# Moving the tensor operations of GpSimd (POOL) to VectorE (DVE) in the last two thirds of a transformer step: output projection and SwiGLU feed-forward

## The chip, the cores and the metric

The program runs on one core of one Trainium2 chip, in one launch. The metric is the device time of one execution in microseconds; lower is better. A core has a matrix engine (PE), a vector engine (DVE), a scalar engine (ACT), a programmable engine (POOL) and a queue engine (SP), each working through its own list of instructions in order, and DMA queues between HBM and the on-chip memory SBUF. Matrix products land in a separate memory, PSUM, from which DVE and ACT read them. An instruction that waits for another engine holds up everything behind it on its own engine.

## The reference

The reference is one inference step of one trunk layer for 128 context tokens and 1024 latent tokens (together T = 1152), width 1024, all in float32. Only its second half matters here; the first (projections, attention, mLSTM scans) is not touched.

```
out = (g_a * (att @ w_o_mla) + g_b * (hm @ w_o_mlstm)) @ w_out
x = x + gt1 * out
h = rmsnorm(x, g_norm_ffn) * (1.0 + sc2) + sh2
a, u = split(h @ w_ffn_in, 2)                  # 2 x 2816 columns
x = x + gt2 * ((silu(a) * u) @ w_ffn_out)
y = rmsnorm(x, g_final)
```

## The kernel before

**Number format.** Every float32 operand of a matrix product is split into a high part (ACT rounds it, method `hi`, line 69) and a low part (DVE subtracts, method `lo`, line 75), and `mm3` (lines 98 to 100) adds three products, high x high, high x low and low x high, so PE's matmuls come in threes on these lines. One `lo` is a DVE subtraction with both inputs in SBUF, and it has to follow its `hi`.

**Layout.** Features lie on the 128 partitions and tokens along the free dimension. The 1152 tokens are two groups g of 576 (`GT`), and each group two halves j of 288 (`HT`); a matmul has 288 columns.

**Stages touched.** They follow one another in this order.

- `merge` (from line 1527): for each feature block it multiplies the attention branch's product by its gate (line 1565), adds the mLSTM branch (line 1566, on POOL) and splits the sum into the operand y of the output projection.
- `w_out` (one call a group): eight feature blocks, two PSUM tiles each of 288 tokens. Each is turned into the new residual stream (`residual`, line 1657) and its square is added to `acc` for the norm (`sq_acc`, line 156, on POOL).
- `h2_ops` (one call a group): `row_rstd` sums `acc` over the partitions (PE, line 135), takes the reciprocal root in a chain of 12 tiny dependent DVE instructions (lines 117 to 123), builds three diagonal tiles `dg` (DVE, line 141), spreads them over the partitions (PE, line 145) and copies them to SBUF (ACT, line 146). Then line 1616 (DVE) scales the four 128x1152 blocks of x, line 1622 (ACT) applies the modulation, lines 1634 to 1644 (POOL) form four differences, and seven operands B11, T1, T2, T3, B22, T4, B21 are split (ACT `th`, DVE `tl`).
- `ffn_in`: the first feed-forward product, in Winograd's form of Strassen's scheme: seven products instead of eight on a 2x2 block pattern. For a weight pair p, `w_ops` makes four sums or differences of weight blocks (lines 1676, 1677, 1682, 1686, on POOL) and seven splits; `pair` runs seven groups of 12 matmuls a token group and combines the PSUM results in seven DVE or ACT instructions (lines 1702 and 1714). ACT applies silu, line 1747 multiplies (POOL), and the result goes to HBM. The 22 pairs come as 28 calls: the first six for g = 0 alone, then the same six for g = 1, then sixteen for both groups.
- `prep`: from the thirteenth call on it forms four sums of the second weight matrix per piece (lines 1772 to 1776, POOL) in 24 pieces, through one load buffer `pr` and one result buffer `ps`, and stores them to HBM as `d_w`.
- `out_ops` and `ffn_out`: the second product, again seven products on a 2x2 pattern, per group. `out_ops` loads the hidden activations, forms 12 differences a group (line 1816, POOL) and splits them; `out_w` splits the weights of each step (three `hi` and three `lo`: 512, 512 and 384 wide); a step is 33 matmuls into one PSUM tile, and there are 28 steps a group. `final` scales the output by the last norm (line 1888, POOL and DVE).

**What sets the order.** The tile framework places the instructions of every engine in an order that it works out for the whole program when the program is built; moving an instruction to another engine can move others too. Buffers are rings: split weights have six tiles (tag `wo`), raw weights four (`wr`), so the splits can run ahead of PE by six tiles: six groups of 12 matmuls in `ffn_in`, two steps in `ffn_out`. PE's products have six PSUM banks. Loads and stores go through SP's queue in order.

Of the kernel before, what the change touches and what calls it, by code (L numbers as in the profile page):

```python
# [14 lines left out]
ALU = mybir.AluOpType  # L15
# [6 lines left out]
KD = 8  # L22
# [26 lines left out]
HT = GT // 2  # L49
# [7 lines left out]
class K:  # L57
# [231 lines left out]
    def inputs(self):  # L289
# [9 lines left out]
        self.wp = self.w2.enter_context(self.pool("w"))  # L299
        self.wb = (4, 4)  # L300
        self.ub = 5
        pp = self.pp = ps.enter_context(self.tc.tile_pool(name="ps1", bufs=1, space=PSUM, reuse_waits="tile"))
# [1227 lines left out]
    def merge(self):  # L1530
# [8 lines left out]
        with pool("ma") as ap:  # L1539
# [8 lines left out]
            for i, (f, g) in enumerate(todo):  # L1548
# [12 lines left out]
                for c in (2 * g, 2 * g + 1):  # L1561
                    self.products(f, c, (3,) if f < 2 else range(4))
                    t = slice(c % 2 * HT, c % 2 * HT + HT)
                    yt = y[g][f][0][:, :, t]
                    nc.vector.tensor_mul(sa[:, t], sa[:, t], self.ps.pop((f, c))[:, :HT])
                    nc.gpsimd.tensor_tensor(t2[:, t], t2[:, t], sa[:, t], op=ALU.add)
                    self.hi(yt[:, 0], t2[:, t])
                    self.lo(yt[:, 1], t2[:, t], yt[:, 0])
# [3 lines left out]
        self.wp = es.enter_context(pool("w2"))  # L1572
        self.wb = (4, 6)
        ar = es.enter_context(pool("ar"))
        self.sp = es.enter_context(pool("st"))
# [9 lines left out]
    def w_out(self, g, y, w0):  # L1585
# [5 lines left out]
        for f in range(KD):  # L1591
# [4 lines left out]
            def evac(p, c0, cw):  # L1596
                b = blk[f // 4][c0 // HT][0]
                self.residual(b[:, f % 4], p, xo[:, c0:c0 + cw], self.mod2[:, 0, f], g * GT + c0, cw)
                self.sq_acc(acc[:, c0:c0 + cw], b[:, f % 4], f == 0, sp, cw, "u2", self.ub, nc.gpsimd)
                nc.sync.dma_start(self.d_x1[f, :, g * GT + c0:g * GT + c0 + cw], b[:, f % 4])  # L1600
# [5 lines left out]
    def h2_ops(self, g, blk, acc):  # L1606

        nc = self.nc
        V, G = nc.vector, nc.gpsimd
        self.row_rstd(acc, acc, D, self.sp, self.pp, "m6", chunks=[(0, HT), (HT, HT)])  # L1610
# [22 lines left out]
        split("B11", b11)  # L1633
        G.tensor_tensor(t1, b12, b11, op=ALU.subtract)
        self.free(s11)
        split("T1", t1)
        G.tensor_tensor(b12, b22, b12, op=ALU.subtract)
        G.tensor_tensor(t1, b22, t1, op=ALU.subtract)
        split("T2", t1)
# [3 lines left out]
        self.free(s22)  # L1643
        G.tensor_tensor(t1, b21, t1, op=ALU.subtract)
        split("T4", t1)
# [17 lines left out]
    def w_ops(self, ra, ru):  # L1663

        nc, wp = self.nc, self.wp
        G = nc.gpsimd
        a11, a12, a21, a22 = ra[:, 0:4], ra[:, 4:8], ru[:, 0:4], ru[:, 4:8]
# [67 lines left out]
    def ffn_in(self, p, groups, last):  # L1735
# [8 lines left out]
        def done(g):  # L1744
            sa, uu = t[g]
            nc.scalar.activation(sa, sa, AF.Silu)
            nc.gpsimd.tensor_tensor(uu, uu, sa, op=ALU.mult)
            nc.sync.dma_start(self.d_g[p, :, g * GT:(g + 1) * GT], uu)
# [8 lines left out]
    def prep(self):  # L1757

        nc, sp = self.nc, self.sp
        G = nc.gpsimd  # L1760
        for p in range(KD // 2):
# [20 lines left out]
    def out_ops(self, g):  # L1782

        nc = self.nc
        G = nc.gpsimd
        B = {}
# [86 lines left out]
    def ffn_out(self):  # L1873
# [3 lines left out]
        for g in range(2):  # L1877
# [3 lines left out]
            def final(j):  # L1881
# [3 lines left out]
                for p in range(KD // 2):  # L1885
                    x = D[p][0][:, j::2]
                    e, r = (nc.vector, bc[:, :HT]) if j == 0 and p < KD // 2 - 1 else (nc.gpsimd, rbc)
                    e.tensor_tensor(x, x, r.unsqueeze(1).broadcast_to([P, 2, HT]), op=ALU.mult)
                    c = g * GT + j * HT
                    ((nc.sync, nc.scalar)[p % 2] if g else nc.scalar).dma_start(self.o["yT"][2 * p:2 * p + 2, :, c:c + HT].rearrange("f p t -> p f t"), D[p][0][:, j::2])  # L1890
# [205 lines left out]
```

## Time and profile before

| what | value |
|---|---|
| median of 3 runs | 2201.28 us (2199.71 to 2201.73) |
| profiled execution | 2201.13 us |
| its span (first to last instruction) | 2199.4 us |
| busy share of the span | PE 94%, DVE 70%, ACT 43%, POOL 45% |

The profile counts an engine as busy from an instruction's start to its end as recorded. The window view gives busy time and number of instructions per engine in a stretch of the span; the group view gives count and mean duration per line and shape; the timeline shows single instructions, with the idle time before them and what ended it in square brackets. Line numbers are those of the kernel before.

### The profile page before, as it was taken

The page shows a single profiled execution, that of the slowest core. Times are in us where ns is not written, and L with a number is a line of the kernel's source. Part 1 is how long each engine was busy: PE and PEld are TensorE (multiplying, and loading weights), DVE is VectorE, ACT ScalarE, POOL GpSimd, SP SyncE. Part 2 cuts the span into 40 slices and gives each one's busy share as a digit, 9 for nine tenths or more (in the row PEclk, how much of TensorE's full clock was granted, in tenths as well). Part 3 has the DMA queues.
Part 4 walks back from the last instruction along what each step waited for, and adds up shares of the span by engine and source line. Part 5 has one row for each costly group of instructions (what it writes and reads, how often), then busy time and mean ns, then how long its engine had stood idle before and what let it go on. Part 6 is the DMA issues. An engine that isn't in the chain of part 4 may idle for free.

```text
span 2199.4 us, 36807 instructions
## 1 busy us (share of the span) xinstructions
PE 2057.0 (94%) x13495; PEld 1873.4 (85%) x13495; DVE 1528.7 (70%) x2700; ACT 935.4 (43%) x1850; POOL 996.6 (45%) x766
## 2 busy tenths in 40 slices
PE   7899989999989888999999999889999999989897
PEld 3689989989978775667776899879999999989897
DVE  3846656988744977566664648899645555799895
ACT  3533334555455534333433335544322222456464
POOL 0622124667435414444446535576776733421501
PEclk9999999999989997999999999899999999999898
DMA  8332335555489685222224664223556512557664
GB/s 314 103 120 83 104 99 162 164 175 187 143 284 326 198 271 153 70 78 71 84 72 116 209 206 145 76 95 123 189 171 196 176 61 85 173 168 253 220 203 129
DMA packets 233795, 343.89 MB, mean 156 GB/s; under 512 B 20079, under 2 KB 166735, under 8 KB 232463
## 3 DMA queue, kind: packets, MB, share of 16 engines
q1 hardware_dynamic: 225070, 331.88, 47.3%
q0 software_dynamic: 4848, 6.06, 1.1%
q10 hardware_dynamic: 3696, 3.61, 0.5%
q8 instruction: 106, 1.74, 0.3%
q14 instruction: 75, 0.61, 0.1%
HBM read 253.69 MB, written 87.80 MB: 155 GB/s over the span
## 4 chain that ended last, share of the span: by engine, by line
PE 47%; DVE 11%; DMA 8%; POOL 6%; issue 5%; ACT 1%; SPq 1%; DVEq 0%; POOLq 0%; ACTq 0%
PE mm L98 11%; PE mm L100 11%; PE mm L99 11%; DVE wo L75 4%; PE pv L1476 3%; DMA pr<-w_fo 3%; PE st L98 2%; PE st L99 1%; PE st L100 1%; PE mx L1398 1%; DVE sm L1400 1%; PE p L1102 1%; PE p L1107 1%; PE p L1104 1%; POOL ps L1773 1%
## 5 line engine op out<-in xcount | busy, mean ns | idle before, releaser
L100 PE MATMUL mm<-th,wo 128*128 128x288 f32 x1840 | 547.3, 298 | 15.1 <-DVE wo L75 14.8
L98 PE MATMUL mm<-th,wo 128*128 128x288 f32 x1840 | 548.7, 298 | 3.0 <-DVE zo L1702 1.1
L99 PE MATMUL mm<-tl,wo 128*128 128x288 f32 x1840 | 547.0, 297 | 0.0
L100 PEld LDWEIGHTS mm<-th,wo 128*128 128x128 f32 x1840 | 349.6, 190 | 19.2 <-DVE wo L75 18.6
L75 DVE TENSOR_TENSOR wo<-wr,wo 128x512 fp32r<-128x512 f32 (+1 forms) x317 | 315.0, 1009 | 54.5 <-ACT wo L69 51.7
L98 PEld LDWEIGHTS mm<-th,wo 128*128 128x128 f32 x1840 | 348.6, 189 | 4.9 <-issue 1.6
L99 PEld LDWEIGHTS mm<-tl,wo 128*128 128x128 f32 x1840 | 349.2, 190 | 0.1
L69 ACT ACTIVATE wo<-wr 128x512 fp32r<-128x512 f32 (+1 forms) x317 | 187.5, 608 | 141.6 <-PE mm L100 62.5
L75 DVE TENSOR_TENSOR wo<-ws,wo 128x512 fp32r<-128x512 f32 x188 | 187.9, 1002 | 64.8 <-ACT wo L69 64.7
L69 ACT ACTIVATE wo<-ws 128x512 fp32r<-128x512 f32 x188 | 116.5, 626 | 270.8 <-PE mm L100 158.1
L1445 POOL TENSOR_TENSOR es<-es,p 128x512 f32<-128x512 f32 x112 | 157.1, 1402 | 91.0 <-ACT p L1438 87.2
L100 PE MATMUL mm<-xh,wo 128*128 128x288 f32 x616 | 184.5, 301 | 9.0 <-DVE wo L75 8.9
L99 PE MATMUL mm<-xl,wo 128*128 128x288 f32 x616 | 184.6, 300 | 0.0
L98 PE MATMUL mm<-xh,wo 128*128 128x288 f32 x616 | 183.9, 299 | 0.2 <-ACT wo L69 0.2
L1686 POOL TENSOR_TENSOR ws<-wr,ws 128x512 f32<-128x512 f32 x47 | 61.8, 1316 | 226.6 <-DVE wo L75 221.2
L1438 ACT ACTIVATE p<-st 128x512 f32<-128x512 f32 (+1 forms) x152 | 87.6, 578 | 158.0 <-PE st L100 146.4
L1400 DVE TENSOR_REDUCE sm<-mx 128x1 f32<-128x384 f32 (+1 forms) x200 | 99.1, 539 | 66.0 <-PE mx L1398 65.1
L98 PE MATMUL mm<-B,wo 128*128 128x288 f32 x456 | 134.8, 296 | 2.2 <-DVE zo L1702 1.3
L100 PE MATMUL mm<-B,wo 128*128 128x288 f32 x456 | 134.8, 296 | 0.0
L99 PE MATMUL mm<-B,wo 128*128 128x288 f32 x456 | 134.8, 296 | 0.0
L722 POOL TENSOR_TENSOR wm<-wm,sr 128x512 f32<-128x512 f32 x64 | 100.8, 1578 | 65.4 <-DVE mj L721 63.4
L100 PEld LDWEIGHTS mm<-xh,wo 128*128 128x128 f32 x616 | 118.0, 192 | 11.5 <-DVE wo L75 11.2
(436 smaller groups left out, 5067.5 us busy)
## 6 DMA issues: line engine op xcount, KB each, us to landing
wr<-w_ff SPq DMA_DIRECT2D x56, 512.0 KB
wm<-wm SPq DMA_DIRECT2D x32, 512.0 KB
wr<-d_w SPq DMA_DIRECT2D x32, 512.0 KB
d_z<-zo SPq DMA_DIRECT2D x48, 288.0 KB
d_g<-uu SPq DMA_DIRECT2D x44, 288.0 KB
wr<-w_big SPq DMA_DIRECT2D x24, 512.0 KB
wr<-w_fo SPq DMA_DIRECT2D x24, 512.0 KB
pr<-w_fo SPq DMA_DIRECT2D x40, 256.0 KB
```

Source lines behind the costliest of these rows:

```text
L69: i = self.nc.scalar.activation(out, in_, AF.Copy)
L75: return self.nc.vector.tensor_sub(out, in_, f32v(hi)).ins
L98: mm(out, lhs[0], rhs[0], start=first, stop=False)
L99: mm(out, lhs[0], rhs[1], start=False, stop=False)
L100: self.pe = mm(out, lhs[1], rhs[0], start=False, stop=last).ins
L722: nc.gpsimd.tensor_tensor(w[:, n], w[:, n], sr[:, 1], op=ALU.mult)
L1102: self.pe = mm(p1, A[:, h], V[:, h], start=True, stop=not carried).ins
L1400: self.iv = nc.vector.tensor_reduce(sm[:, t, j:j + 1], s[:, :kc], axis=AX.X, op=ALU.max, negate=True).ins
L1438: self.ia = nc.scalar.activation(p[:, :n], st[:, :n], AF.Exp).ins
L1445: nc.gpsimd.tensor_tensor(U["sum"], U["sum"], p, op=ALU.add)
L1476: self.pe = nc.tensor.matmul(pv[g * AV:(g + 1) * AV, q0:q0 + w], v[:, kb[c]], U["P"][c][:, q0:q0 + w], start=c < 2, stop=c == U["nc"] - 1, ...
L1686: G.tensor_tensor(s4, a12, s2, op=ALU.subtract)
```

## The change

All tensor operations that POOL did from `merge` on go to DVE: the additions in `merge`, the sums of squares in `w_out`, the four differences in `h2_ops`, the weight sums of `w_ops` (through a field `G`, which is POOL in the earlier stages and DVE from here), the silu product, the sums of `prep`, the differences of `out_ops` and the scalings of `final`, except one scaling in the last group that stays on POOL. What is computed stays the same.

```diff
@@ inputs
         self.wb = (4, 4)
+        self.G = self.nc.gpsimd
         self.ub = 5
@@ merge
-                    nc.gpsimd.tensor_tensor(t2[:, t], t2[:, t], sa[:, t], op=ALU.add)
+                    nc.vector.tensor_add(t2[:, t], t2[:, t], sa[:, t])
...
         self.wb = (4, 6)
+        self.G = nc.vector
@@ w_out
-                self.sq_acc(acc[:, c0:c0 + cw], b[:, f % 4], f == 0, sp, cw, "u2", self.ub, nc.gpsimd)
+                self.sq_acc(acc[:, c0:c0 + cw], b[:, f % 4], f == 0, sp, cw, "u2", self.ub)
@@ h2_ops
-        G.tensor_tensor(t1, b12, b11, op=ALU.subtract)
+        V.tensor_tensor(t1, b12, b11, op=ALU.subtract)
...
-        G.tensor_tensor(b12, b22, b12, op=ALU.subtract)
-        G.tensor_tensor(t1, b22, t1, op=ALU.subtract)
+        V.tensor_tensor(b12, b22, b12, op=ALU.subtract)
+        V.tensor_tensor(t1, b22, t1, op=ALU.subtract)
...
-        G.tensor_tensor(t1, b21, t1, op=ALU.subtract)
+        V.tensor_tensor(t1, b21, t1, op=ALU.subtract)
@@ w_ops
-        G = nc.gpsimd
+        G = self.G
@@ ffn_in
-            nc.gpsimd.tensor_tensor(uu, uu, sa, op=ALU.mult)
+            nc.vector.tensor_mul(uu, uu, sa)
@@ prep
-        G = nc.gpsimd
+        G = nc.vector
@@ out_ops
-        G = nc.gpsimd
+        G = nc.vector
@@ ffn_out
-                    e, r = (nc.vector, bc[:, :HT]) if j == 0 and p < KD // 2 - 1 else (nc.gpsimd, rbc)
+                    e, r = (nc.gpsimd, rbc) if g and j == 0 and p == KD // 2 - 1 else (nc.vector, rbc if j else bc[:, :HT])
```

Up to the products of `merge` the engines' lists are the same. Behind them two places matter below. In the changed kernel, lines from 1576 on carry a number higher by two.

The first place is PE's list where the feed-forward part goes over from group 0 to group 1. `m6_2592` is the spread reciprocal root of group 1's second half of tokens (`row_rstd` in `h2_ops`), made from the diagonal tiles `dg_2591`. The products `mm_2757`, `mm_2760` and `mm_2763` are the first three of group 1, with the operands B11, T2 (`th_2598`) and T1 (`th_2596`, `tl_2597`). Before:

```order
L100 MATMUL mm_2672_14518<-th_2506_13501,wo_2671_14515 128x288
L145 MATMUL m6_2592_14114<-dg_2591_14110,ones_65 128x128 x2
L145 MATMUL m6_2592_14114<-dg_2591_14110,ones_65 128x32
L98 MATMUL mm_2672_14518<-th_2506_13501,wo_2671_14515 128x288
L99 MATMUL mm_2672_14518<-tl_2507_13502,wo_2671_14515 128x288
```

In the changed kernel:

```order
L99 MATMUL mm_2757_15017<-tl_2595_14141,wo_2756_15014 128x288
L100 MATMUL mm_2757_15017<-th_2594_14140,wo_2756_15014 128x288
L145 MATMUL m6_2592_14114<-dg_2591_14110,ones_65 128x128 x2
L145 MATMUL m6_2592_14114<-dg_2591_14110,ones_65 128x32
L98 MATMUL mm_2760_15035<-th_2598_14151,wo_2759_15032 128x288
L98 MATMUL mm_2763_15053<-th_2596_14145,wo_2762_15050 128x288
```

The spread stood in the third call for group 0, 306 rows ahead of the first matmul on T2; now it stands directly in front of that matmul, behind all of group 0's calls.

DVE's list at the same place, before. `x1_2515` and `x1_2517` are group 1's residual blocks of the second half of tokens, which line 1616 scales.

```order
L1702 TENSOR_TENSOR uu_2645_14372<-uu_2645_14372,mm_2655_14433 128x288
L75 TENSOR_TENSOR wo_2673_14533<-wr_2656_14450,wo_2673_14533 128x512
L141 TENSOR_SCALAR dg_2591_14110<-ident_60,y_2589_14096 128x128 x3
L1702 TENSOR_TENSOR u2_2665_14492<-m1_2662_14474,mm_2664_14479 128x288
L75 TENSOR_TENSOR wo_2676_14552<-ws_2675_14550,wo_2676_14552 128x512
L75 TENSOR_TENSOR wo_2678_14569<-wr_2657_14452,wo_2678_14569 128x512
L75 TENSOR_TENSOR wo_2684_14597<-wr_2680_14589,wo_2684_14597 128x512
L1702 TENSOR_TENSOR sa_2668_14510<-u2_2665_14492,mm_2667_14497 128x288
L1616 TENSOR_TENSOR x1_2515_13519<-x1_2515_13519,acc_2518_13522 128x1152
L1616 TENSOR_TENSOR x1_2517_13521<-x1_2517_13521,acc_2518_13522 128x1152
```

In the changed kernel:

```order
L1749 TENSOR_TENSOR uu_2741_14928<-uu_2741_14928,sa_2740_14927 128x576
L122 TENSOR_TENSOR t_2590_14097<-t_2590_14097,v_2588_14095 128x3
L123 SCALAR_TENSOR_TENSOR y_2589_14096<-t_2590_14097,y_2589_14096 128x3
L141 TENSOR_SCALAR dg_2591_14110<-ident_60,y_2589_14096 128x128 x3
L1618 TENSOR_TENSOR x1_2515_13519<-x1_2515_13519,acc_2518_13522 128x1152
L1618 TENSOR_TENSOR x1_2517_13521<-x1_2517_13521,acc_2518_13522 128x1152
L1636 TENSOR_TENSOR t1_2593_14139<-x1_2515_13519,x1_2514_13518 128x1152
L1639 TENSOR_TENSOR x1_2515_13519<-x1_2517_13521,x1_2515_13519 128x1152
L75 TENSOR_TENSOR tl_2597_14146<-t1_2593_14139,th_2596_14145 128x1152
L75 TENSOR_TENSOR tl_2603_14160<-x1_2517_13521,th_2602_14159 128x1152
L1640 TENSOR_TENSOR t1_2593_14139<-x1_2517_13521,t1_2593_14139 128x1152
L75 TENSOR_TENSOR tl_2601_14156<-x1_2515_13519,th_2600_14155 128x1152
```

The diagonals moved from the second call for group 0 to a place behind the silu product of its sixth and last call (`uu_2741`), and the four differences and the operand splits, which were spread over POOL's and DVE's lists, now follow in one block.

The second place is the change from the first to the second product. Before, POOL's list has the differences of group 0's hidden activations and the last two silu products in one run, while DVE's list at that time holds splits only:

```order
L1747 TENSOR_TENSOR uu_3491_19832<-uu_3491_19832,sa_3490_19831 128x576
L1816 TENSOR_TENSOR t1_3510_19931<-gr_3539_20077,t1_3510_19931 128x1152
L1816 TENSOR_TENSOR gr_3504_19895<-gr_3539_20077,gr_3504_19895 128x1152
L1747 TENSOR_TENSOR uu_3494_19848<-uu_3494_19848,sa_3493_19847 128x576
L1816 TENSOR_TENSOR t1_3509_19930<-gr_3538_20075,t1_3509_19930 128x1152
L1816 TENSOR_TENSOR gr_3503_19893<-gr_3538_20075,gr_3503_19893 128x1152
```

In the changed kernel DVE's list has:

```order
L1818 TENSOR_TENSOR t1_3510_19931<-gr_3539_20077,t1_3510_19931 128x1152
L1818 TENSOR_TENSOR gr_3504_19895<-gr_3539_20077,gr_3504_19895 128x1152
L1704 TENSOR_TENSOR uu_3494_19848<-uu_3494_19848,mm_3520_19993 128x288
L75 TENSOR_TENSOR wo_3545_20093<-wr_3533_20029,wo_3545_20093 128x384
L1818 TENSOR_TENSOR t1_3509_19930<-gr_3538_20075,t1_3509_19930 128x1152
L1818 TENSOR_TENSOR gr_3503_19893<-gr_3538_20075,gr_3503_19893 128x1152
L75 TENSOR_TENSOR wo_3552_20142<-wr_3541_20083,wo_3552_20142 128x512
L1749 TENSOR_TENSOR uu_3491_19832<-uu_3491_19832,sa_3490_19831 128x576
```

The same operations now stand between the weight splits (`wo`) that PE's next steps need, on the engine that makes those splits.

More of the change, by code (lines that the diff above doesn't have):

```diff
@@ L1608, in h2_ops @@
         nc = self.nc
-        V, G = nc.vector, nc.gpsimd
+        V = nc.vector
         self.row_rstd(acc, acc, D, self.sp, self.pp, "m6", chunks=[(0, HT), (HT, HT)])
```

## The prediction

> **What bounds the kernel now.** I read the page's first part, then the window view with its matmul counts from `merge` to the end, then the waits of PE in the stretches that fall short, and last what DVE and POOL do in them. Columns of the window view: length, then busy time and number of instructions of PE, PEld, DVE, ACT and POOL, granted PE clock, DMA share, GB/s.
>
> ```profile
> PE 2057.0 (94%) x13495; PEld 1873.4 (85%) x13495; DVE 1528.7 (70%) x2700; ACT 935.4 (43%) x1850; POOL 996.6 (45%) x766
> ```
> ```profile
> 1240.00:1370.00 130.00, 130.00 (x987) 130.00 (x986) 85.10 (x143) 56.03 (x104) 61.34 (x52) 1.00 0.61 188
> 1375.00:1475.00 100.00, 80.25 (x524) 76.19 (x524) 93.45 (x120) 47.81 (x81) 66.56 (x37) 0.90 0.25 82
> 1475.00:1550.00 75.00, 73.82 (x553) 73.37 (x552) 70.37 (x94) 30.40 (x57) 53.81 (x37) 1.00 0.42 137
> 1550.00:1800.00 250.00, 248.59 (x1858) 247.54 (x1857) 143.12 (x236) 69.32 (x126) 165.99 (x162) 1.00 0.50 163
> 1800.00:1875.00 75.00, 75.00 (x565) 75.00 (x564) 41.14 (x73) 21.07 (x36) 24.06 (x18) 1.00 0.20 69
> 1900.00:1950.00 50.00, 41.34 (x277) 39.28 (x276) 47.27 (x37) 20.57 (x37) 33.55 (x13) 0.93 0.64 193
> 1950.00:2050.00 100.00, 99.22 (x747) 98.76 (x746) 93.73 (x169) 66.05 (x116) 16.83 (x8) 1.00 0.72 228
> 2050.00:2075.00 25.00, 16.02 (x92) 15.43 (x91) 23.68 (x31) 6.86 (x15) 17.76 (x7) 0.73 0.51 163
> 2075.00:2175.00 100.00, 99.63 (x751) 99.40 (x750) 84.51 (x144) 66.00 (x114) 8.90 (x3) 1.00 0.64 201
> ```
>
> PE is the bound, and undisturbed it does 565 matmuls in 75 us, 7.53 a us (0.133 us each). Against that rate the stretches lose (753 - 524) / 7.53 = 30.4 us in 1375 to 1475, 1.6 up to 1550, (1883 - 1858) / 7.53 = 3.3 in 1550 to 1800, (377 - 277) / 7.53 = 13.3 in 1900 to 1950, 0.8 up to 2050, (188 - 92) / 7.53 = 12.8 in 2050 to 2075 and 0.3 after it: 62.5 us, the most that this change could win. In the stretches that lose much, DVE is busy over 93% and POOL is busy too. `merge` and `w_out` (1240 to 1370) lose nothing.
>
> DVE's group view of a stretch where POOL stands almost still (2100 to 2175), then of 1400 to 1475, then one row of 1900 to 1945:
>
> ```profile
> L75 DVE TENSOR_TENSOR wo<-wr,wo 128x512 fp32r<-128x512 f32 x36 | 24.4, 686 | 7.7 <-ACT wo L69 7.5
> L75 DVE TENSOR_TENSOR wo<-wr,wo 128x384 fp32r<-128x384 f32 x18 | 9.9, 552 | 0.0
> L75 DVE TENSOR_TENSOR xl<-gr,xh 128x1152 fp32r<-128x1152 f32 x4 | 5.4, 1354 | 0.0
> ```
> ```profile
> L75 DVE TENSOR_TENSOR wo<-wr,wo 128x512 fp32r<-128x512 f32 x14 | 19.9, 1442 | 0.0
> L75 DVE TENSOR_TENSOR tl<-x,th 128x1152 fp32r<-128x1152 f32 x4 | 8.5, 2129 | 0.0
> L1702 DVE TENSOR_TENSOR u<-m,mm 128x288 f32<-128x288 f32 x5 | 2.2, 441 | 0.0
> ```
> ```profile
> L75 DVE TENSOR_TENSOR wo<-wr,wo 128x512 fp32r<-128x512 f32 x12 | 22.0, 1861 | 0.0
> ```
>
> The same subtraction of 512 columns takes 0.69 us without POOL and 1.44 or 1.86 us beside it; the addition that reads PSUM stays at 0.44 us. So the long DVE rows are waits for POOL, not work. DVE's timeline at its worst and POOL's groups behind it (1890 to the end, then 1340 to 1550):
>
> ```profile
> 1910.51 21.26 DVE L75 TENSOR_TENSOR wo<-wr,wo 128x384 fp32r<-128x384 f32 x10
> ```
> ```profile
> L1816 POOL TENSOR_TENSOR t<-gr,t 128x1152 f32<-128x1152 f32 x8 | 24.5, 3062 | 13.6 <-DVE wo L75 10.6 <-ACT wo L69 3.0
> ```
> ```profile
> L1682 POOL TENSOR_TENSOR ws<-wr,wr 128x512 f32<-128x512 f32 x13 | 23.1, 1781 | 2.4 <-DVE wo L75 2.4
> ```
>
> Ten weight splits, about 6 us alone, last 21 us.
>
> **What an operation costs on DVE.** From 0.686 us (512) and 1.354 us (1152) follow 1.04 ns a column; neighbouring rows overlap by about 0.08 us, so the seat on DVE is 0.60 us at 512 and 1.27 at 1152, by the same slope 0.35 at 256 and 0.67 at 576; 0.47 at 384 and 0.37 for the 288 wide addition by their own rows. POOL's 1.8 and 3.1 us fall away.
>
> **Calls for one group (1375 to 1550).** A call has 84 matmuls, 11.15 us. On DVE it has 7 splits and 4 moved sums of 512, 7 PSUM operations (a few on ACT) and a product of 576: 11 x 0.60 + 7 x 0.37 + 0.67 = 9.9 us. The list puts 64.0 us of DVE work by these seats (with group 1's first normalisation) beside the six calls for group 0, 66.9 us of PE. That fits, at 96%; I allow 4 us of small stalls, between 0 and 10. Then the new order bites. Rows for its price: the tail's chain (DVE, ACT), line 1616 twice without POOL, line 1622 eight times, one `hi` of 1152.
>
> ```profile
> 2189.88 0.68 DVE L141 TENSOR_SCALAR dg<-ident,y 128x128 f32<-128x128 f32 x3
> 1331.41 2.63 DVE L1616 TENSOR_TENSOR x<-x,acc 128x1152 f32<-128x1152 f32 x2 [0.47 <-ACT acc L146]
> ```
> ```profile
> 2191.81 0.40 ACT L146 COPY rbc<-m 128x288 f32<-128x288 f32 x1 [5.27 <-PE m L145]
> 1347.71 4.27 ACT L1622 ACTIVATE x<-x,mod,A 128x288 f32<-128x288 f32 x8 [2.76 <-DVE x L1616]
> 1353.50 1.15 ACT L69 ACTIVATE th<-x 128x1152 fp32r<-128x1152 f32 x1
> ```
>
> Between the last addition of call six and the end of `dg` stand 8 operations of 512, the product, one addition, the small ones and `dg`: 7.1 us, of which 12 matmuls on B11 cover 1.6. PE waits at the spread for 5.5 us. Then, with PE's next matmul on T2 waiting for all of it: `dg` to the end of the copy 1.65 us (2190.56 to 2192.21), the first of line 1616 1.3, line 1622 on both blocks 4.3, second difference, two low splits and the difference T2 4 x 1.27 = 5.1, its `hi` 1.15: 13.5 us. Together PE stands for 19 us; between 10, if DVE comes early, and 23, if ACT's other splits get in between.
>
> What a standstill costs behind it, from PE's timeline:
>
> ```profile
> 1384.98 1.44 PE L135 MATMUL m<-ones,acc 128*128 128x1 f32 x6 [6.01 <-POOL acc L156]
> ...
> 1386.91 0.44 PE L98 MATMUL mm<-th,wo 128*128 128x288 f32 x1
> ...
> 1391.23 0.44 PE L98 MATMUL mm<-th,wo 128*128 128x288 f32 x1
> ```
> ```profile
> 2069.56 1.46 PE L145 MATMUL m<-dg,ones 128*128 128x128 f32 x6 [7.68 <-DVE dg L141]
> ...
> 2074.09 0.41 PE L100 MATMUL mm<-xh,wo 128*128 128x288 f32 x1
> ```
>
> Behind 6.01 us PE runs at about 0.24 us a matmul until 1391.5, some 22 matmuls at 0.107 us too much, 2.3 us; behind 7.68 us the half rate ends by 2074.3, 1.8 us. So the slow time doesn't grow with the wait; I add 2.3 us. The Trainium skill says the same in "TensorE: Matmul & The Clock Gate", section "What's actually happening": half clock after an idle window of about 3.4 us, full clock after one busy window; a cost that grew with the wait would add about 7 us to mine instead of 2.3. The trace's stretches at half rate (6.6 and 4.8 us with the first small matmuls) are longer than one window but agree in that.
>
> Sum for this stretch: 19 + 2.3 + 4 + 1.5 (T4 and B21 of the same block come late too) = 27 us lost, against 32.0 before: a gain of 5.
>
> **Prep (1550 to 1800).** POOL's timeline around one piece:
>
> ```profile
> 1562.33 1.07 POOL L1776 TENSOR_TENSOR ps<-pr,ps 128x256 f32<-128x256 f32 x1
> 1568.38 0.73 POOL L1772 TENSOR_TENSOR ps<-pr 128x256 f32<-128x256 f32 x1 [4.97 <-DMA pr<-w_fo]
> ```
>
> With one buffer `pr`, the next piece can start 5 us after the last sum of the one before. POOL sat these out; now DVE does, with everything behind it: splits and additions that PE needs. In the list stand on average 3.8 us of other DVE work between two pieces, so it stands for about 1.2 us, 24 times, 29 us. DVE's work in the nine calls for both groups around it is 16 to 17.6 us a call against 22.3 of PE, so some 47 us are free, and PE has six tiles of lead. I take 5 us lost instead of 3.3; between 0 and 30.
>
> **Second product.** 56 steps of 33 matmuls are 245 us of PE. DVE's list from there on is 219 us by these seats, 24 differences (16 of 1152 and 8 of 864, 28 us in all) and seven more scalings included. Step by step it stays within the two steps of lead but once: in group 1's first steps four scalings and four differences (4 x 0.67 + 2 x 1.27 + 2 x 0.97 = 7.2 us) and then two more stand ahead of weights, behind a spread: 1.8 + 7.2 + 0.6 = 9.6 us against 8.8 of lead, and 1.5 more for the next split. 2.3 us and 2 of half clock behind it. So 4.4 instead of 26.9 us: a gain of 22.5, between 10 and 27.
>
> **The rest.** `merge` and `w_out` take 30 additions and 28 of 288 (0.37 us); DVE is busy 65% there, with POOL's 61 us falling away, and PE keeps its work: 0; uncovered they would cost 21 us. At the end, final scalings of half j = 1 stand ahead of the last residual on DVE, but within PE's last step, which lies between the last two residuals:
>
> ```profile
> 2179.93 0.52 DVE L1657 SCALAR_TENSOR_TENSOR d<-mm,mod,d 128x288 f32<-128x288 f32 x1 [2.24 <-PE mm L100]
> 2184.98 0.52 DVE L1657 SCALAR_TENSOR_TENSOR d<-mm,mod,d 128x288 f32<-128x288 f32 x1 [2.25 <-PE mm L100]
> ```
>
> 4.5 us for them: 0, between 0 and 2.
>
> Sum: 2201.1 (the profiled execution, 0.1 us under the median) - 5 + 1.7 - 22.5 = 2175.
>
> **Rivals.**
>
> *The entry wait is not there*: DVE runs ahead of PE and the normalisation is done in time, or what PE waits for is shorter. For it: DVE has slack; against it: the diagonals stand behind the silu product of call six, which needs PE's last product. It gives 2175 - 21 = 2154.
>
> *The second product's splits wait for weights, not for POOL.* For it, a row of the groups from 1000 on:
>
> ```profile
> L69 ACT ACTIVATE wo<-wr 128x512 fp32r<-128x512 f32 (+1 forms) x260 | 151.7, 603 | 104.5 <-PE mm L100 30.0 <-DMA wr<-d_w 29.0 <-issue 18.0
> ```
>
> ACT's splits waited for loads from `d_w`, 29 us. Against it: raw weight buffers come free only when DVE has read them. Half of 22.5 lost again: 2186, up to 2190.
>
> *Prep binds (slower).* DVE stands at the loads, and PE runs out of tiles. A piece now takes 5 + 2.2 us of sums and interleaved splits = 7.2 us, 24 of them 173 us, in 190 us of PE. If a load comes 2 us later than 5, that is 9.2 x 24 = 221 us: 31 us more, 2206. It decides from about 5.7 us on.
>
> *The long DVE rows are DVE's own work (slower).* To DVE's 163.8 us of 1375 to 1550 come the moved sums and products, 14 calls of 3.1 us (4 x 0.60 + 0.67), 43 us, with 175 us of room: 32 us more, and no gains elsewhere, 2230. The rows beside POOL against those without it speak against it. The Trainium skill advises in "Perfetto Trace Analysis", section "Optimizing Scalar/DVE Operations", to move work away from a saturated DVE, to GpSimd too, which by itself speaks against this change; it adds that the shared SBUF port may spoil that.
>
> **How the numbers follow.** The forecast (2165 to 2186) has 0.62, no entry wait 0.14, half the gain 0.14, prep 0.07, own work 0.03. The range leaves out the two slower cases and some of the lowest: 2153 to 2196. Within 0.2% (4.4 us, what a measurement tells from no change) lies the edge of half the gain and a mild prep, 0.04; slower 0.07; faster 0.89.
>
> **What would show it.** Right: weight splits of 512 at 0.69 us everywhere after 1375; no waits like 6.01 and 7.68 us; 1900 to 1950 near 375 matmuls; one PE wait of 10 to 23 us in two pieces, at line 145 and at the first T2 matmul, between the sixth and the seventh call. Wrong: several PE waits for DVE within prep, or DVE rows as long as before.

## The result, and the profile after

The changed kernel takes 2170.03 us (median of 4 runs, 2166.79 to 2179.29) against 2201.51 us before (4 runs): a ratio of 0.9864, 95% interval 0.983 to 0.9897. Timed a second time (first experiment) it took 2170.81 us, ratio 0.9858 (0.9838 to 0.9877). The forecast was 2175 us.

The window view of the changed kernel, with the columns and the stretches of the one shown before:

```profile
1240.00:1370.00 130.00, 130.00 (x987) 130.00 (x986) 95.29 (x195) 57.00 (x105) 0.00 (x0) 1.00 0.59 184
1375.00:1475.00 100.00, 81.40 (x598) 81.06 (x597) 91.48 (x178) 53.79 (x92) 0.00 (x0) 0.90 0.29 97
1475.00:1550.00 75.00, 75.00 (x565) 75.00 (x564) 69.28 (x136) 32.22 (x55) 0.00 (x0) 1.00 0.50 162
1550.00:1800.00 250.00, 247.82 (x1852) 246.76 (x1851) 180.53 (x383) 67.99 (x121) 0.00 (x0) 1.00 0.47 151
1900.00:1950.00 50.00, 48.63 (x362) 48.03 (x362) 44.74 (x66) 31.91 (x53) 0.00 (x0) 1.00 0.67 213
2050.00:2075.00 25.00, 23.49 (x173) 22.79 (x172) 21.12 (x29) 15.03 (x26) 0.00 (x0) 1.00 0.72 243
```

POOL does nothing there. PE does 362 matmuls instead of 277 in 1900 to 1950 and 173 instead of 92 in 2050 to 2075. DVE's groups in 1400 to 1475, and one row of 1900 to 1945, show the durations that the prediction took from stretches without POOL:

```profile
L75 DVE TENSOR_TENSOR wo<-ws,wo 128x512 fp32r<-128x512 f32 x19 | 12.8, 684 | 0.5 <-ACT wo L69 0.5
L75 DVE TENSOR_TENSOR wo<-wr,wo 128x512 fp32r<-128x512 f32 x14 | 9.4, 684 | 0.0
L1749 DVE TENSOR_TENSOR uu<-uu,sa 128x576 f32<-128x576 f32 x5 | 3.8, 752 | 0.3 <-ACT sa L1748 0.3
L1679 DVE TENSOR_TENSOR ws<-ws,wr 128x512 f32<-128x512 f32 x5 | 3.4, 685 | 0.0
```
```profile
L75 DVE TENSOR_TENSOR wo<-wr,wo 128x512 fp32r<-128x512 f32 x22 | 14.7, 685 | 4.7 <-ACT wo L69 4.7
```

The split of 512 columns takes 0.68 us where it took 1.44 and 1.86. And PE's timeline has the new wait in two pieces, between the sixth call for group 0 and the first for group 1:

```profile
1451.30 1.46 PE L145 MATMUL m<-dg,ones 128*128 128x128 f32 x6 [6.04 <-DVE dg L141]
1465.32 0.85 PE L98 MATMUL mm<-th,wo 128*128 128x288 f32 x2 [12.57 <-ACT th L69]
1465.96 0.44 PE L99 MATMUL mm<-tl,wo 128*128 128x288 f32 x1
...
1468.36 0.44 PE L100 MATMUL mm<-th,wo 128*128 128x288 f32 x1
```

PE first waits 6.04 us for the diagonals and then 12.57 us for the high part of T2; behind it, for 3.3 us, matmuls take 0.44 us each and start 0.24 us apart instead of 0.133.

To set stages rather than windows side by side, I counted products in PE's timeline: the first feed-forward product has 3696 and the second 1848 of 288 columns. The table has the time between the starts of the 1st, 504th (six calls for group 0), 1008th (group 1, in most kernels), 2520th (nine calls for both, beside `prep`) and last of the first, then from the first to the 925th of the second product and from there to PE's end, in microseconds. In e8 and e9 three calls for both groups stand between those for group 0 and group 1: there the column of six calls for g = 1 holds these three calls, and the next column six calls for g = 1 and six for both. Each row is one profiled execution, the median beside it is of all runs. The last row is 7.53 products a microsecond, the rate before.

| kernel | start | six calls g = 0 | six calls g = 1 | nine for both | seven for both | second product, half 1 | half 2 to PE's end | median of the runs |
|---|---|---|---|---|---|---|---|---|
| before | 1375.1 | 100.7 | 68.3 | 204.8 | 156.8 | 139.0 | 147.0 | 2201.5 |
| changed | 1374.4 | 69.0 | 89.0 | 205.0 | 156.8 | 126.0 | 136.8 | 2170.0 |
| e1 changed, again | 1374.2 | 69.0 | 89.2 | 205.2 | 156.8 | 128.1 | 135.9 | 2170.8 |
| e2 early normalisation | 1376.3 | 84.9 | 67.1 | 212.5 | 156.8 | 128.1 | 138.7 | 2168.1 |
| e3 weight sums on POOL | 1377.1 | 83.8 | 70.0 | 212.9 | 156.8 | 127.9 | 137.8 | 2175.1 |
| e4 differences on POOL | 1377.8 | 69.0 | 88.9 | 205.8 | 156.8 | 140.0 | 146.4 | 2195.0 |
| e5 probe | 1378.8 | 90.6 | 90.3 | 204.8 | 156.8 | 125.3 | 137.1 | 2188.1 |
| e6 prep on POOL | 1371.1 | 69.0 | 89.3 | 205.3 | 157.8 | 126.4 | 137.1 | 2175.1 |
| e7 early, two load buffers | 1379.1 | 84.9 | 67.1 | 201.6 | 156.8 | 128.5 | 139.1 | 2165.0 |
| e8 as e7, mixed calls | 1374.9 | 84.8 | 67.2 | 201.6 | 156.8 | 128.2 | 137.0 | 2159.1 |
| e9 as e8, late operands | 1376.9 | 81.9 | 67.2 | 201.6 | 156.8 | 126.5 | 141.3 | 2159.5 |
| e10 before, differences on DVE | 1374.8 | 100.7 | 68.4 | 205.8 | 156.8 | 126.1 | 140.5 | 2187.8 |
| e11 before, normalisation on DVE | 1379.3 | 90.0 | 67.7 | 205.2 | 156.8 | 139.5 | 147.2 | 2193.4 |
| without a stall | | 66.8 | 66.9 | 200.8 | 156.2 | 122.7 | | |

The spans of the two profiled executions differ by 2199.4 - 2165.0 = 34.4 us: 31.7 less in the calls for group 0, 20.7 more in those for group 1, 13.0 and 10.2 less in the two halves of the second product; the start, `prep` and the tail make up the other 0.2. The changed kernel's profiled execution took 2166.79 us; the medians differ by 31.5 us.

### The profile page after: what moved, and what is told of

Same layout as the page of the kernel before. It is cut to its first block, busy times and chain, and to the rows that moved or that the text cites. A ratio compares the mean times of both kernels' runs of the same rounds, so it can differ in the third digit from the quotient of the medians.

```text
span 2165.0 us, 36550 instructions
## 1 busy us (share of the span) xinstructions
PE 2036.3 (94%) x13495; PEld 1858.1 (86%) x13495; DVE 1558.4 (72%) x3053; ACT 940.4 (43%) x1850; POOL 521.8 (24%) x413
## 3 DMA queue, kind: packets, MB, share of 16 engines
q10 hardware_dynamic: 3696, 3.61, 0.5%
## 4 chain that ended last, share of the span: by engine, by line
PE 53%; DVE 10%; DMA 9%; issue 3%; ACT 2%; POOL 1%; SPq 1%; DVEq 0%; ACTq 0%; POOLq 0%
PE mm L98 13%; PE mm L100 13%; PE mm L99 13%; DMA pr<-w_fo 4%; PE pv L1477 3%; DVE wo L75 2%; PE st L98 2%; PE st L100 1%; PE st L99 1%; PE mx L1399 1%; DVE sm L1401 1%; PE p L1103 1%; PE p L1105 1%; PE p L1108 1%; POOL wm L723 1%
## 5 line engine op out<-in xcount | busy, mean ns | idle before, releaser
L75 DVE TENSOR_TENSOR wo<-wr,wo 128x512 fp32r<-128x512 f32 (+1 forms) x317 | 228.4, 734 | 51.5 <-ACT wo L69 48.5
L98 PE MATMUL mm<-xh,wo 128*128 128x288 f32 x616 | 181.9, 296 | 1.8 <-ACT wo L69 1.8
L100 PE MATMUL mm<-xh,wo 128*128 128x288 f32 x616 | 179.8, 295 | 1.7 <-DVE wo L75 1.7
L75 DVE TENSOR_TENSOR wo<-ws,wo 128x512 fp32r<-128x512 f32 x188 | 140.3, 748 | 21.2 <-ACT wo L69 21.1
L98 PEld LDWEIGHTS mm<-xh,wo 128*128 128x128 f32 x616 | 115.5, 188 | 2.8 <-ACT wo L69 2.7
L100 PEld LDWEIGHTS mm<-xh,wo 128*128 128x128 f32 x616 | 115.1, 188 | 2.5 <-DVE wo L75 2.4
```

What stands on the lines that cost most here:

```text
L75: return self.nc.vector.tensor_sub(out, in_, f32v(hi)).ins
L98: mm(out, lhs[0], rhs[0], start=first, stop=False)
L100: self.pe = mm(out, lhs[1], rhs[0], start=False, stop=last).ins
```

## The experiments

**e1, the changed kernel again.**

> The changed kernel once more, for a second trace and for its scatter (2167 to 2179 so far). Theory: PE's wait at the entry to group 1 comes back in two pieces of about 6.0 us (line 145) and 12.6 us (first T2 matmul), the six calls for group 0 take 69 us and those for group 1 89 us, since they follow from the order of the lists. If the wait was an accident of one execution, one of the pieces is missing or shorter by several us.

Measured: 2170.81 us (2167.07 to 2174.5), and PE's gaps are 6.04 and 12.57 us again, to the hundredth. The wait belongs to the order of the lists.

**e4 and e10: the differences of the second product, undone and alone.** e4 is the changed kernel with them back on POOL (the edit shown), e10 the kernel before with only them on DVE (the reverse edit):

```diff
     def out_ops(self, g):
...
-        G = nc.vector
+        G = nc.gpsimd
```

> Changed kernel, but the 24 differences of hidden activations are back on POOL. Theory (port): each of them holds up DVE's splits again for some 2 to 3 us; the first half of the second product goes from 126.0 back to 134 to 139 us and the second half from 136.8 to 142 to 147, with splits of 512 at 1.5 us and more beside them; time 2182 to 2193. Rival (those splits waited for weights from memory, and the gain came from the order): both halves stay within 2 us, time 2168 to 2172.

> Kernel before with one part of the change alone: the 24 differences of hidden activations on DVE. Theory (what that part brings is local and adds to the rest): the two halves of the second product go from 139.0 and 147.0 us to 126 to 129 and 136 to 139, the stages ahead stay as before, time 2176 to 2182. Rival (the gain there needs the rest of the change, since weight splits also meet POOL's silu products and scalings): the halves fall by under 15 us together, time 2186 or more.

Measured: e4 takes 2194.95 us (2189.73 to 2196.71), 24.1 us more than the changed kernel beside it; e10 takes 2187.77 us (2182.53 to 2191.74), ratio 0.9933 (0.9912 to 0.9954). In the table the two halves lose 12 to 14 and 10 us again in e4, and gain 12.9 and 6.5 in e10. DVE's groups of e4 in 1900 to 1945, POOL's longest group of e4 from 1890 on, and DVE in the same stretch of e10:

```profile
L75 DVE TENSOR_TENSOR wo<-wr,wo 128x512 fp32r<-128x512 f32 x15 | 16.4, 1117 | 5.2 <-ACT wo L69 5.2
L75 DVE TENSOR_TENSOR wo<-wr,wo 128x384 fp32r<-128x384 f32 x8 | 10.2, 1272 | 0.6 <-ACT wo L69 0.6
L1749 DVE TENSOR_TENSOR uu<-uu,sa 128x576 f32<-128x576 f32 x2 | 6.4, 3214 | 0.0
```
```profile
L1818 POOL TENSOR_TENSOR t<-gr,t 128x1152 f32<-128x1152 f32 x8 | 24.4, 3063 | 43.4 <-DMA gr<-d_g 41.6 <-ACT xh L69 1.8
```
```profile
L75 DVE TENSOR_TENSOR wo<-wr,wo 128x512 fp32r<-128x512 f32 x17 | 11.2, 687 | 3.4 <-ACT wo L69 3.4
```

With the differences on POOL, splits of 384 columns take 1.27 us and a silu product 3.2 us instead of 0.75; with them on DVE a 512 wide split takes 0.69 us although the rest is as before. PE's wait for split weights in the second product, in e4 and then in the changed kernel:

```profile
PE mm L100 <- DVE wo L75: 15.9, 8, 5.0
```
```profile
PE mm L100 <- DVE wo L75: 1.7, 3, 0.8
```

That the gain hung on weights from memory is refuted: no load was edited, and the time went and came with the differences. Both edits change DVE's list as well as POOL's load, so the rows show the contention, but not how much of the time is order; e5 below leaves the order as it is. In size the expectations missed in places: e4 is longer than I said (2182 to 2193), with a mean split of 1.12 us and not 1.5, and e10's second half takes 140.5 us where I had 136 to 139. e10's runs scatter over 9 us: its profiled execution (2182.53) shows 19.4 us of gain in the two halves, the median only 13.6 altogether, which is the time of the rival. Where its longer runs lose, no trace shows.

**e5, the price of POOL's occupancy by itself.** 40 subtractions on POOL for nobody; the lists of PE, DVE and ACT are the changed kernel's, row by row.

```diff
+            if i == 0:
+                scr = sp.tile([P, 512], F32, name=self.nm("scr"), tag="scr")
+                nc.gpsimd.tensor_copy(scr, self.h2[0]["T4"][0].rearrange("p k t -> p (k t)")[:, :512].bitcast(F32))
+                for _ in range(40):
+                    nc.gpsimd.tensor_tensor(scr, scr, scr, op=ALU.subtract)
             self.ffn_in(p, g, i == len(todo) - 1)
```

> Changed kernel plus 40 subtractions 128x512 on POOL on a scratch tile of their own, started as the six calls for group 0 begin; nobody waits for them, and the order of PE, DVE and ACT is the same row by row. Theory (POOL's tensor operation and DVE's operations with both inputs in SBUF hold each other off): beside them the 512 wide splits take 1.3 us or more instead of 0.69, the PSUM additions stay at 0.45, the 40 take some 1.8 us each, and the six calls for group 0 go from 69 us to 85 us or more, time 2185 to 2205. Rival (the losses before came from results of POOL that came late, not from its being busy): DVE's rows stay, the six calls stay at 69 us, time 2170.

Measured: 2188.12 us (2186.34 to 2193.54), and 90.6 us for the six calls instead of 69.0. DVE's groups in 1376 to 1440 and POOL's, then five rows of the changed kernel in the same place (1374 to 1440):

```profile
L75 DVE TENSOR_TENSOR wo<-ws,wo 128x512 fp32r<-128x512 f32 x12 | 13.9, 1156 | 0.0
L156 DVE TENSOR_TENSOR acc<-acc,sq 128x288 f32<-128x288 f32 x7 | 7.2, 1050 | 0.0
L1659 DVE SCALAR_TENSOR_TENSOR x<-mm,mod,xo 128x288 f32<-128x288 f32 x4 | 1.9, 506 | 0.0
L121 DVE SCALAR_TENSOR_TENSOR t<-y 128x3 f32<-128x3 f32 x3 | 1.8, 590 | 0.0
L1704 DVE TENSOR_TENSOR u<-m,mm 128x288 f32<-128x288 f32 x4 | 1.8, 442 | 0.0
L119 DVE TENSOR_SCALAR y<-t 128x3 int32<-128x3 int32 x1 | 1.0, 1002 | 0.0
```
```profile
L1982 POOL TENSOR_TENSOR scr<-scr 128x512 f32<-128x512 f32 x40 | 54.1, 1353 | 3.1
```
```profile
L75 DVE TENSOR_TENSOR wo<-ws,wo 128x512 fp32r<-128x512 f32 x21 | 14.2, 684 | 0.5 <-ACT wo L69 0.5
L1704 DVE TENSOR_TENSOR u<-m,mm 128x288 f32<-128x288 f32 x6 | 2.7, 452 | 2.0 <-PE mm L100 2.0
L156 DVE TENSOR_TENSOR acc<-acc,sq 128x288 f32<-128x288 f32 x5 | 2.2, 454 | 0.0
L121 DVE SCALAR_TENSOR_TENSOR t<-y 128x3 f32<-128x3 f32 x4 | 0.6, 151 | 0.0
L119 DVE TENSOR_SCALAR y<-t 128x3 int32<-128x3 int32 x2 | 0.3, 160 | 0.0
```

This is the contention by itself: no result of POOL is waited for, yet the split goes from 0.68 to 1.16 us (I had expected 1.3), the sum of squares from 0.45 to 1.05, and the tiny step on y (three columns, both inputs y from SBUF) from 0.15 to 0.59, while what takes one input from PSUM stays at 0.44 and 0.51. POOL's own subtractions take 1.35 us (expected: 1.8). 21.6 us for 54 us of POOL is 0.4 us lost by PE per microsecond of POOL, in a stretch where DVE is then busy all 90.6 us. The Trainium skill has this in "SBUF — State Buffer", section "Who interferes with whom": a DVE instruction with two inputs in SBUF contends with a GpSimd instruction that reads SBUF, one with at most one such input doesn't, outside the two-port modes. The rows named so far agree. Two kinds of row with one tensor input in SBUF don't fit the plain rule: line 119 took 1.00 us here (a single instruction) instead of 0.16, and a diagonal (line 141) took 0.99 us in the kernel before and 0.28 in the changed one (1374 to 1480):

```profile
L141 DVE TENSOR_SCALAR dg<-ident,y 128x128 f32<-128x128 f32 x6 | 5.6, 992 | 0.0
```
```profile
L141 DVE TENSOR_SCALAR dg<-ident,y 128x128 f32<-128x128 f32 x6 | 1.4, 281 | 0.0
```

Whether these ran in a two-port mode, no run here shows.

**e3, the weight sums back on POOL.**

```diff
         self.wb = (4, 6)
-        self.G = nc.vector
+        self.G = nc.gpsimd
```

> Changed kernel, but the four weight sums of a call are back on POOL. Theory (POOL's tensor operations hold off DVE's subtractions with both inputs in SBUF): the 512 wide splits in the twelve calls for one group go from 0.69 to 1.3 us or more, PSUM additions stay at 0.45, the six calls for group 0 go from 69 to 90 us or more; the calls for both groups stay hidden; time 2182 to 2197. Rival (the long rows are DVE's own load): DVE is rid of 12 x 4 x 0.60 = 29 us and the twelve calls get shorter, time 2150 to 2165.

Measured: 2175.07 us (2170.39 to 2176.55), 4.3 us more than the changed kernel beside it: neither theory's time. The splits were held, though less than I had said; DVE's groups in the twelve calls:

```profile
L75 DVE TENSOR_TENSOR wo<-ws,wo 128x512 fp32r<-128x512 f32 x45 | 39.6, 886 | 0.0
L75 DVE TENSOR_TENSOR wo<-wr,wo 128x512 fp32r<-128x512 f32 x36 | 36.5, 1022 | 0.0
```
```profile
1413.81 0.83 PE L145 MATMUL m<-dg,ones 128*128 128x128 f32 x6 [0.40 <-DVE dg L141]
```

81 splits lose (39.6 + 36.5) - 81 x 0.684 = 20.7 us, and DVE is rid of 12 x 4 x 0.60 = 29 us of sums. My expectation counted the first without the second. And moving the sums moved the order too: the spread of group 1's second half stands early (1413.81, against 1451.30 in the changed kernel), so the entry wait is gone and the twelve calls take 153.8 us, 4 us less than in the changed kernel. The nine calls behind them take 7.9 us more; DVE stands 61.6 us at the loads of `prep` there and PE waits 7.8 us for DVE's additions, much as in e2 below. Against e2, which has the sums on DVE and no entry wait either, e3's twelve calls are 1.8 us longer: as far as two lists in different order can be compared, the move of the sums alone is worth little for these calls, since what it spares in contention it puts on DVE as work.

**e11, the squares and the differences of the normalisation alone, on the kernel before.**

```diff
-                self.sq_acc(acc[:, c0:c0 + cw], b[:, f % 4], f == 0, sp, cw, "u2", self.ub, nc.gpsimd)
+                self.sq_acc(acc[:, c0:c0 + cw], b[:, f % 4], f == 0, sp, cw, "u2", self.ub)
...
-        V, G = nc.vector, nc.gpsimd
+        V = G = nc.vector
```

> Kernel before with another part alone: the squares in the output projection and the four differences of the normalisation on DVE; weight sums and silu products stay on POOL. Theory (part of the loss was that POOL's list brought the sum of squares late): the wait of 6.0 us at line 135 is gone, the twelve calls for one group go from 169.0 us to 155 to 163, time 2187 to 2196. Rival (only the sums and the splits beside them count): they stay at 166 to 170 us, time 2198 to 2202.

Measured: 2193.38 us (2188.86 to 2198.83), ratio 0.9961 (0.9949 to 0.9972); the twelve calls take 157.7 us instead of 169.0. PE's waits in them, of the kernel before and of e11:

```profile
PE mm L100 <- DVE wo L75: 11.2, 7, 5.5
PE m L135 <- POOL acc L156: 6.0, 1, 6.0
PE m L145 <- DVE dg L141: 2.9, 3, 1.4
```
```profile
PE mm L100 <- DVE wo L75: 5.8, 7, 2.5
PE mm L98 <- DVE sa L1702: 3.1, 3, 1.1
PE m L145 <- DVE dg L141: 2.7, 1, 2.7
```

The 6.0 us were a wait for POOL's result: on POOL the last addition of squares, some 1.2 us long, stood behind weight sums and differences. Whether POOL's operations ahead of it were longer for DVE's sake, this run doesn't separate. Stage and time are as expected.

**e2, the entry wait taken away.** The diagonals and spreads of group 1 are ordered ahead of calls of group 0, nothing else is changed. `self.nrm` holds the last diagonal and spread of each half, `self.tsp` the splits of T2.

```diff
...
+            if i == 0:
+                (d0, s0), (d1, s1) = self.nrm
+                behind = {2: (d0,), 3: (s0, d1), 4: (s1,), 5: self.tsp['T2']}
+            with contextlib.ExitStack() as es:
+                for x in behind.get(i, ()):
+                    es.enter_context(self.tc.issue_after(x))
+                self.ffn_in(p, g, i == len(todo) - 1)
```

> Changed kernel, but the order is forced: group 1's diagonals and spread stand ahead of the third to fifth call for group 0, and the split of T2 ahead of the sixth. Theory (the entry wait is an order of the list, the chain of tiny DVE steps stands behind larger ones): the waits of 6.0 and 12.6 us at the entry are gone; DVE has 12 calls x 9.9 us and some 25 us of normalisation, 144 us, against 134 of PE and about 8 of lead, so a part comes back as small stalls: the twelve calls take 142 to 148 us instead of 158, time about 2156 (2150 to 2162). Rival (DVE's sum binds, so the wait is only spread): the twelve calls stay at 155 to 160 us, time 2168 to 2172.

Measured: 2168.05 us (2166.34 to 2173.82), the rival's time, but not for the rival's reason alone. The two waits are gone, and the twelve calls take 152.0 us instead of 158.0, between theory and rival, while the nine calls beside `prep` take 212.5 instead of 205.0. (The profiled execution took 2173.82 us, 5.8 more than the median.) DVE in e2's six calls (windows), then PE's and DVE's waits in the nine calls (1528 to 1741), and DVE's in the changed kernel's (1532 to 1738):

```profile
1400.00:1420.00 20.00, 17.42 (x117) 15.40 (x117) 19.42 (x43) 13.65 (x27) 0.00 (x0) 1.00 0.20 68
1420.00:1440.00 20.00, 15.77 (x87) 15.54 (x88) 20.00 (x29) 13.35 (x21) 0.00 (x0) 0.74 0.20 68
1440.00:1461.00 21.00, 19.98 (x145) 19.08 (x144) 21.00 (x36) 9.24 (x17) 0.00 (x0) 1.00 0.44 143
```
```profile
PE mm L98 <- DVE sa L1707: 6.1, 5, 2.6
PE mm L98 <- DVE uu L1707: 2.1, 2, 1.9
```
```profile
DVE ps L1777 <- DMA pr<-w_fo: 49.1, 21, 5.6
```
```profile
DVE ps L1774 <- DMA pr<-w_fo: 42.4, 21, 5.2
```

DVE is full from 1400 to 1461 (60.4 of 61 us): with the wait gone, its own work looks like the limit, and e8 and e9 below try that. And in the nine calls PE waits 8.2 us for DVE's additions (`sa`, `uu`), which free PSUM banks, while DVE stands at the loads for 49 us. The changed kernel's DVE stands there almost as long, and PE waits only 2.1 us for these additions: there they fall better.

**e6 and e7: what the loads of `prep` cost.** e6 is the changed kernel with the sums of `prep` on POOL (`G = nc.gpsimd` there). e7 is e2 with two buffers for the load and smaller pieces, 208 columns instead of 256:

```diff
...
-                r = sp.tile([P, 2, 2, 256], F32, name=self.nm("pr"), tag="pr")
+                r = sp.tile([P, 2, 2, 208], F32, name=self.nm("pr"), tag="pr", bufs=2)
...
```

> Changed kernel, but the sums of prep are back on POOL; PE's order stays as it is. Theory (the loads' waits on DVE are hidden by six tiles of lead in this order, and 256 wide sums on POOL hold DVE little): DVE's 42 us of waits for pr go to POOL, the first nine calls for both groups take 204 to 206 us as with the sums on DVE, time 2168 to 2173. Rival (the waits on DVE cost PE time): 201 to 202 us, time 2166 to 2168.

> The forced early order of the normalisation, and two load buffers for prep instead of one, with pieces of 208 columns (28 pieces instead of 24). With the early order and one buffer the nine calls took 212.5 us. Theory (there DVE stood at the loads while PE waited for its PSUM additions): DVE's waits for pr fall from 49 to under 15 us and the nine calls take 203 to 206 us, twelve calls 152 as before, time 2161 to 2165. Rival (the stretch is longer because PE comes into it with no tiles ahead, whatever the loads do): 209 us or more, time 2167 to 2170.

Measured: e6 2175.12 us (2165.69 to 2182.04), ratio 0.9878 (0.9842 to 0.9914), a median above both expectations, with runs 16 us apart. Its profile, of the run of 2165.69 us, has 205.3 us for the nine calls, as the theory said. But DVE isn't free there: the queue engine now stands at POOL's sums, whose stores it issues, and the stores of the hidden activations `uu` behind them come late. DVE's and the queue's longest waits in the nine calls of e6:

```profile
DVE uu L1704 <- DMA d_g<-uu: 41.1, 7, 8.6
```
```profile
SPq L1779 <- POOL ps L1778: 138.4, 23, 9.5
```

So e6 put another wait of DVE in the place of the first, and what the loads cost in the changed kernel stays open, up to the 4.2 us that its nine calls lie above no stall. e7 takes 2164.96 us (2160.36 to 2166.46), ratio 0.9828 (0.9803 to 0.9852), and the nine calls 201.6 us, 10.9 less than in e2's profiled execution and 0.8 above no stall. DVE's waits there:

```profile
DVE ps L1777 <- DMA pr<-w_fo: 13.3, 6, 3.8
DVE ps L1777 <- DMA d_w<-ps: 12.1, 11, 2.9
```

So in e2's order the loads do cost, and a second buffer takes that away: PE has no wait in e7's nine calls. By their medians e7 is only 3.1 us under e2, and the intervals overlap, so the 10.9 us hold for the two traces. There is now some waiting for the result buffer too, which PE doesn't see.

**e8 and e9: what limits the six calls for group 0.** e8 is e7 with three calls for both groups between those for group 0 and group 1; `prep` starts three calls later. e9 is e8 with group 1's operands T3, B22, T4 and B21 made behind group 0's six calls (`self.late`; `dv` and `av` are the last silu product and silu of the sixth call).

```diff
-        todo = [(p, (0,)) for p in range(self.NA)] + [(p, (1,)) for p in range(self.NA)] + \
-            [(p, (0, 1)) for p in range(self.NA, NF)]
+        both = [(p, (0, 1)) for p in range(self.NA, NF)]
+        todo = [(p, (0,)) for p in range(self.NA)] + both[:3] + [(p, (1,)) for p in range(self.NA)] + both[3:]
...
-            if i == 12:
+            if i == 15:
...
+            if i == self.NA:
+                with self.tc.issue_after(self.dv), self.tc.issue_after(self.av):
+                    for _ in self.late:
+                        pass
...
```

> As the run with the early order and two buffers, but three calls for both groups (13.1 us of DVE against 22.3 of PE) come between the six for group 0 and the six for group 1 (9.9 against 11.15 each). Theory (DVE's sum binds in the twelve calls: it was never idle there): group 1's later operands and the tiles ahead are made in those calls, and PE loses under 10 us from the start of the feed-forward part to the end of the six calls for group 1, instead of 18; time 2153 to 2160. Rival (the loss sits in the six calls for group 0 itself): the same as without it, 2161 to 2165.

> As the run with three calls for both groups in between, and T3, B22, T4 and B21 of group 1 (five DVE operations of 1.27 us, 6.4 us) are made only behind group 0's six calls. With the early order those six calls took 84.8 us, as long as DVE's own work there: 6 x 9.9 + 25 of normalisation = 84.4. Theory (DVE's sum sets the length of the six calls): they take 78 to 80 us, the next 504 matmuls 67 to 69, time 2152 to 2158. Rival (it is the order of the list, not the sum): the six calls stay at 84 to 86 us, time 2157 to 2163.

Measured: e8 2159.1 us (2156.34 to 2165.04), ratio 0.9811 (0.9786 to 0.9837); e9 2159.48 us (2157.05 to 2162.94), ratio 0.9807 (0.9792 to 0.9823). e8's median is one that the theory named, but the stage decides: its six calls take 84.8 us as before and what follows has no loss, as in e7. The loss sits in the six calls, as the rival said. Its profiled execution lies 5.1 us under e7's (2161.22 against 2166.36), and 4.2 of them are the start of the feed-forward part, ahead of the edit; I can't call e8 faster than e7. e9's six calls take 81.9 us, between the two expectations: of 6.4 us of DVE work moved away 2.9 come back. But DVE's busy time in the six calls fell only from 81.4 to 78.2 us, since operations of 512 columns from later on moved up into the room. So e9 doesn't separate the amount of DVE's work from its order. Nor does its total fall: its last stage takes 4.3 us more than e8's, and why is open. e9's windows:

```profile
1400.00:1420.00 20.00, 17.89 (x123) 15.97 (x121) 19.41 (x43) 13.08 (x26) 0.00 (x0) 1.00 0.19 68
1420.00:1440.00 20.00, 15.80 (x92) 14.89 (x92) 20.00 (x31) 11.98 (x21) 0.00 (x0) 0.83 0.21 68
1440.00:1455.00 15.00, 15.00 (x115) 15.00 (x114) 14.70 (x29) 7.04 (x13) 0.00 (x0) 1.00 0.51 161
```

DVE is full from 1400 to 1440 here too, where the normalisation's block stands, and there PE falls short; from 1440 on it doesn't. How much an even spread would bring is open. e8 and e9 are 1.9% under the kernel before and 0.5% under the changed kernel of e1; their intervals lie just below e1's (0.9838 to 0.9877) and overlap that of the first timing (0.983 to 0.9897).

## Why the prediction was right

Forecast 2175 (range 2153 to 2196), measured 2170. Step by step:

**The cause** (long DVE rows are waits for POOL) was right: e5 makes long rows by POOL's occupancy alone, with the other lists as they were, and e4 and e10 undo and make the gain of the second product in its place. It wasn't the whole loss: by e11, 6.0 us and the half rate behind them came from a POOL result that stood in a queue. The rival of DVE's own work is refuted in its price: it put 43 us more on DVE and 32 on PE (which gives 2233, not 2230); DVE's rows fell to 0.68 us.

**The seats on DVE** (0.60 at 512 and so on) were right: by them 64.0 us of DVE work stood beside the six calls for group 0, and DVE is busy 65.2 of their 69.0 us. PE has no wait there. The 69.0 - 66.8 = 2.2 us are the 18 small matmuls of the normalisation between the products (18 / 7.53 = 2.4), so of the 4 us of stalls that I allowed none came.

**The entry wait** was right in place and order, and nearly in size: 5.5 us foretold at the spread, 6.04 measured; 13.5 from the diagonals to the first T2 matmul, which holds the spread itself, against 1.46 + 12.57 = 14.0. The chain behind the diagonals stands in the trace step by step as foretold. The six calls for group 1 lose 89.0 - 66.9 = 22.1 us, where I had 19 + 2.3 + 1.5 = 22.8. That these sums agree so well is partly luck: beside the waits of 18.6 us stand 1.5 of the spread and 1.4 of half rate (13 matmuls at 0.107), and no wait for the late operands that I put at 1.5 shows in the trace. Behind the wait of 12.57 us the half rate lasts no longer than behind 6 us before, so here too it doesn't grow with the wait. The rival without this wait is refuted.

**The mis-sized term** is the gain in this stretch: 5 us in the text, 35.3 - 24.3 = 11.0 us by stages. What failed is "32.0 before" and the 4 us of stalls. The 32.0 came from counting all matmuls of 1375 to 1550 as products of 0.133 us; 24 of them were the small ones of the normalisation (lines 135 and 145), 24 / 7.53 = 3.2 us that were a loss as well: 100.7 + 68.3 - 133.7 = 35.3 us by stages. The other part is the 27 us after: 69.0 + 89.0 - 133.7 = 24.3.

**Prep**: 1.7 us more foretold, 0.2 measured. DVE stood at the loads 42.4 us, 2.0 each time, where I had 1.2. The sign that I had named for being wrong, several PE waits for DVE here, shows in small: four, 2.1 us in all. The reason given, six tiles of lead, leaves out a path: in e2 PE meets the stop through the additions that free PSUM banks, and that trace pays 10.9 us more than e7's. So what the rival feared, DVE standing at the loads and PE behind it, does occur in another order, at a third of its price; but through PSUM banks, not because PE runs out of tiles, and without its condition (a load over 5.7 us).

**Second product**: 22.5 us of gain foretold, 23.2 measured (22.0 in e1). The hitch foretold in group 1's first steps (4.3 us) is about 2 us: 173 of 188 matmuls in 2050 to 2075. In 1900 to 1950 stand 362 matmuls where I had said near 375. The rival of half this gain is refuted by both halves and by e10's trace; e10's median alone wouldn't refute it.

**The rest**: `merge` and `w_out` at 0: 987 matmuls in 130 us before and after, with DVE at 95 us instead of 85. The tail costs 0.4.

## What to carry to other kernels

Before sharing elementwise work between DVE and POOL, compare the same DVE row in stretches with and without POOL: a busy DVE may only be held off, and long POOL operations are best kept away from stretches in which the matrix engine waits for DVE's subtractions. Then read the new order for what stands behind what: here the change won 55 us in three stages and gave 20.7 back in one, because a chain of tiny steps and a block of long ones came at the last moment. Taking such a wait away shows the next limit, here a full DVE and, in the new order, a single load buffer, and each needs a step of its own.

## What was not expected

Tiny DVE operations can lose as much time as long ones: in e5 the three-column step of line 121 took 0.59 us instead of 0.15, while a 512 wide split went from 0.68 to 1.16. It isn't so wherever POOL is busy: in the kernel before the same step took 0.16 us on average.

The start of the feed-forward part, ahead of which PE, DVE and ACT have the same lists in the changed kernel, e1, e4 and e6, lies between 1371.1 and 1377.8 us. So some 7 us of the scatter between runs of these kernels are made ahead of the stages that the variants change, and single times of variants are compared better by stage.

The two pieces of the entry wait agree to a hundredth of a microsecond in the five profiled executions that have this order at this place (changed kernel, e1, e4, e5 and e6): here a wait that comes from the order of the lists doesn't scatter.
